# Two-layer transformer step on one core: attention scores of two heads issued as one alternating group on the two 64-row halves

## The chip, the cores and the metric

The kernel runs on one core of a Trainium2 chip, as one program with one launch. The metric is the device time of that program in microseconds (us), as the median of repeated runs, and less is better.

## The reference, cut to what matters

Two transformer blocks work on 512 tokens of width 1024. The change touches the three places where scores of queries against keys are made, all with 64 features to a head:

```python
# first block, 4 heads, each with two score maps (n = 0, 1)
scores = jnp.einsum('bhnqd,bhnkd->bhnqk', qb, kb) * scale
probs = jax.nn.softmax(jnp.where(mask, scores, -jnp.inf), axis=-1)
attn = probs[:, :, 0] - lam * probs[:, :, 1]
...
# second block, 8 index heads: which keys each query may see
dots = jnp.einsum('bqhd,bsd->bqhs', qi, k_idx)
score = jnp.einsum('bqh,bqhs->bqs', wi, jax.nn.relu(dots))
_, idx = lax.top_k(score, topk)
...
# second block, 8 attention heads over the latent keys
logits = jnp.einsum('bqhc,bqkc->bqhk', ql, c_sel) * ATT_SCALE + bias
probs = jax.nn.softmax(logits, axis=-1)
```

Everything else (projections, feed-forward layers, a gated recurrence, norms) is left as it is.

## The kernel before, in words

All activations lie in SBUF as tiles of 128 features by 512 tokens. A product in float32 is made of three products in float32r: each operand is split into a high and a low part (`split`), and high x high, high x low and low x high are added up in one PSUM bank. So a weight block of 1024 features is 24 matmuls of 512 columns.

Scores are made by `dots` (line 583): for one head, one block of 128 queries and the L keys up to that block (L = 128, 256, 384 or 512), three matmuls with 64 rows each. Two heads share a tile: one lies on rows 0 to 63, the other on rows 64 to 127. Below, A is a matmul on the lower half, B one on the upper half, and a number behind it is L / 128: A4 is a matmul of 512 columns on the lower half. A triple is the three matmuls of one head. There are 264 such matmuls:

- `attention` (line 800, phase `mixa`), four heads with two maps each: 24 matmuls of each L. Behind each triple, VectorE takes the row maximum and ScalarE the exponential.
- `select_keys` (line 1053, phase `mixb`), eight heads, L = 256, 384, 512: 24 of each. Behind each, ScalarE takes the relu and VectorE adds it to the score; then VectorE picks the greatest keys, 16 rounds of maximum and replacement to a block.
- `latent_attention` (line 1089, phase `mixb`), eight heads: 24 of each L. Behind each triple come two VectorE operations, an exponential, transposes on TensorE, a copy on ScalarE and the product with the values. `self.sm("lg", LOGITS)` takes the bank of these scores, and at most LOGITS = 3 banks hold them at a time.

PSUM has eight banks, shared by all products (`mm` for blocks of weights, `sm` for the rest). Nothing is written in the order in which it runs. `Plan.add` records each operation with a cost; `Plan.simulate` is a list scheduler over five engines, the PSUM banks and the buffers; `write` (the call is on line 444, which is why every instruction has that line in the profile) puts the operations out in the order found. Products that are ready early, above all the 16 blocks of the two gates (`w2gate`), fill TensorE between the small steps of the second block's mix. `nc.group` ties matmuls of one group into a chain: each waits its turn behind the one before it, though others may be put between them.

Of the kernel before, what the change touches and what calls it, by code (L numbers as in the profile page):

```python
# [15 lines left out]
PSUM = bass.MemoryType.PSUM  # L16
DRAM = bass.MemoryType.DRAM

P = 128
# [7 lines left out]
LEAD, PACE, LOGITS = {True: 14000, False: 6000}, 1500, 3  # L27
# [10 lines left out]
class View:  # L38
    """a tile, or a part of one, that gets its place when the program is written out"""
# [85 lines left out]
class Base:  # L125
# [5 lines left out]
    def halve(self, at):  # L131
        """from here on the columns before and behind this one are written and read apart"""
        self.at, self.parts = at, [Part(), Part()]
# [27 lines left out]
class Plan:  # L161
    """records instructions, orders them by a model of the core's engines, then writes them out"""
# [8 lines left out]
    def add(self, engine, call, args, kw):  # L171
# [41 lines left out]
        else:  # L213
# [3 lines left out]
            if engine == "tensor":  # L217
                r = all(v.base.dt == F32R for v in ins)
                wide = args[1].n
                o.cost = 3 + (128 * 2 if call == "transpose" else max(n, 2 * wide) if r else 4 * max(n, wide)) / 2.4  # L220
            elif engine == "scalar":
# [15 lines left out]
    # ordering  # L237
# [12 lines left out]
    def simulate(self, first):  # L250
        """list scheduling: sets o.start; the order of starts"""
# [195 lines left out]
class Net:  # L447
# [8 lines left out]
    # tiles  # L456
# [28 lines left out]
    # constants  # L485
    def setup(self):
# [16 lines left out]
        for _ in range(WARM):  # opens the clock gate of the array  # L503
            nc.tensor.matmul(p, self.ident, self.ident, start=True, stop=True)
# [5 lines left out]
    def later(self):  # L510
        """what the first products do not wait for"""
# [14 lines left out]
    def held(self, w, K, behind):  # L526
        """like chunk(), in slots: the parts of K blocks"""
# [21 lines left out]
    # weights: two float32r parts whose sum is the float32 weight  # L549
# [15 lines left out]
    def split(self, x, g=None, to=None):  # L565
        """x (times the column g) in two float32r parts"""
# [16 lines left out]
    def dots(self, p, q, k, s, t, L):  # L583
        """queries t..L on partitions, keys before L"""
        (qh, ql), (kh, kl) = q, k
        for i, (x, y) in enumerate(((qh, kh), (qh, kl), (ql, kh))):
            self.nc.tensor.matmul(p, x[s, t:L], y[s, :L], start=i == 0, stop=i == 2)

    def block(self, xs, w, p=None):
        """one block of 128 output features in PSUM; w: [P, K * 128] in DRAM"""  # L590
# [12 lines left out]
    def both(self, xs, ws, ps, held=None):  # L603
        """blocks of 128 output features: step by step all of them for one half of the tokens"""
# [16 lines left out]
    def tokens(self, xs, w, n, whole=False, cut=False):  # L621
        """n output features, tokens on partitions: four PSUM banks; w: [chunks, P, k * n]; whole: so many blocks of
        tokens at a time; cut: the last block by halves of the features"""
# [34 lines left out]
    # norms; with a side: for one half of the tokens  # L658
# [858 lines left out]
```

## Time and profile before

| what | value |
|---|---|
| median of the three runs | 1773.06 us (1772.69 to 1775.02) |
| span of the profiled execution | 1772.8 us; it has no other time of its own |
| TensorE (PE) busy | 1759.4 us, 99% |
| weight loads (PEld) busy | 1476.8 us, 83% |
| VectorE (DVE) busy | 1033.4 us, 58% |
| ScalarE (ACT) busy | 715.1 us, 40% |
| DMA | 162.47 MB, 92 GB/s on the mean |

The span runs from the first to the last instruction of one execution; what a run has around it is the difference to the median, 0.2 us. A matmul's busy time in the profile is longer than its turn, since the next one starts while it drains; the distance from start to start is its cost. A row that names `64*128` is a matmul with 64 rows, `128*128` one with all rows.

### The profile page before, as it was taken

To read this page: it belongs to the slowest core of one execution; us is meant where nothing else is said; L and a number is where in the kernel's file an instruction comes from. 1 tells how busy PE (TensorE), PEld (TensorE's weight loads), DVE (VectorE), ACT (ScalarE), POOL (GpSimd) and SP (SyncE) were. 2 spreads that over 40 slices of the span, in tenths; PEclk is the share of its full clock that TensorE was granted. 3 is DMA by queue.
4 is the path that set the end of the run, shared out by engine and by line. 5 is a ranking of instruction groups with operands and counts; after the bars stand their busy time and mean duration, and the time that the engine had idled before them with its cause. 6 is when DMAs were issued, how large, how long until landed. Compare 5 with 4: busy or idle time off the path is not lost.

```text
span 1772.8 us, 22576 instructions
## 1 busy us (share of the span) xinstructions
PE 1759.4 (99%) x8882; PEld 1476.8 (83%) x8882; DVE 1033.4 (58%) x1820; ACT 715.1 (40%) x1248; POOL 49.3 (3%) x68
## 2 busy tenths in 40 slices
PE   9999999999999999999999999999999999999998
PEld 7778888888888888888898888788899888888896
DVE  7886776367655432343488999553657432343475
ACT  5664444234443322322355334553345322322364
POOL 0021000000000000000010000000000000000000
PEclk9999999999999999999999999999999999999999
DMA  5212232332233223332342321013331323322331
GB/s 201 72 53 92 94 96 77 113 107 96 77 103 106 95 73 106 107 97 83 111 130 71 95 84 49 13 48 95 97 130 49 104 75 101 112 95 80 113 105 60
DMA packets 51690, 162.47 MB, mean 92 GB/s; under 512 B 5936, under 2 KB 7552, under 8 KB 51584
## 3 DMA queue, kind: packets, MB, share of 16 engines
q1 hardware_dynamic: 51584, 161.04, 28.9%
q8 instruction: 69, 1.13, 0.3%
q14 instruction: 37, 0.30, 0.1%
HBM read 158.89 MB, written 2.12 MB: 91 GB/s over the span
## 4 chain that ended last, share of the span: by engine, by line
PE 94%; DVE 4%; ACT 0%; issue 0%; DMA 0%; SPq 0%; POOL 0%; POOLq 0%; DVEq 0%; ACTq 0%
PE ffn.mm L444 41%; PE ffna.mm L444 20%; PE mixb.mm L444 15%; PE mixa.mm L444 7%; PE mixb.sm L444 5%; PE ple.mm L444 3%; DVE mixb.slot L444 2%; PE mixa.sm L444 2%; DVE mixb.m L444 0%; PE ffn.sm L444 0%; DMA mixa.wr_52:2_113<-in_w1qk 0%; SPq L444 0%; PE ple.sm L444 0%; PE fin.sm L444 0%; DVE mixa.dsum L444 0%
## 5 line engine op out<-in xcount | busy, mean ns | idle before, releaser
L444 DVE TENSOR_TENSOR ffn.slot<-ffn.slot,ffn.mm 128x512 f32<-128x512 f32 (+1 forms) x68 | 42.4, 625 | 177.2 <-PE ffn.mm L444 176.5
L444 DVE TENSOR_TENSOR ffn.slot<-ffn.mm,ffn.slot 128x512 f32<-128x512 f32 x44 | 30.3, 691 | 110.4 <-PE ffn.mm L444 109.6
L444 PE MATMUL mixb.sm<-mixb.slot,mixb.slot 128*128 128x64 f32 (+6 forms) x496 | 73.6, 308 | 1.0 <-ACT mixb.slot L444 0.5
L444 DVE TENSOR_TENSOR mixb.slot<-mixb.slot,mixb.slot 128x256 f32<-128x256 f32 (+3 forms) x143 | 67.3, 495 | 11.6 <-ACT mixb.slot L444 11.0
L444 PEld LDWEIGHTS mixb.sm<-mixb.slot,mixb.slot 128*128 128x128 f32 (+1 forms) x496 | 61.1, 190 | 12.2 <-issue 3.3
L444 DVE SCALAR_TENSOR_TENSOR ffna.slot<-ffna.slot,cols,ffna.slot 128x511 f32<-128x511 f32 x88 | 65.8, 748 | 3.1 <-ACT ffna.slot L444 1.3
L444 DVE TENSOR_TENSOR ffna.slot<-ffna.mm,ffna.slot 128x512 f32<-128x512 f32 x44 | 30.3, 689 | 46.4 <-PE ffna.mm L444 45.8
L444 ACT ACTIVATE ffn.slot<-ffn.slot 128x512 f32<-128x512 f32 (+1 forms) x68 | 39.2, 578 | 40.0 <-DVE ffn.slot L444 39.8
L444 DVE TENSOR_TENSOR ffn.slot<-ffn.slot,ffn.slot 128x512 fp32r<-128x512 f32 (+2 forms) x94 | 52.0, 562 | 5.0 <-ACT ffn.slot L444 4.6
L444 ACT COPY mixb.slot<-mixb.sm 128x128 f32<-128x128 f32 (+6 forms) x75 | 27.1, 376 | 43.3 <-PE mixb.sm L444 43.0
L444 DVE TENSOR_TENSOR ffna.slot<-ffna.slot,ffna.slot 128x512 f32<-128x512 f32 (+1 forms) x51 | 35.3, 691 | 14.7 <-ACT ffna.slot L444 13.8
L444 DVE TENSOR_TENSOR mixb.slot<-mixb.mm,mixb.slot 128x512 f32<-128x512 f32 (+1 forms) x28 | 19.3, 690 | 41.7 <-PE mixb.mm L444 40.5
L444 ACT ACTIVATE ffna.slot<-ffna.slot,cols 128x512 f32<-128x512 f32 x44 | 35.8, 815 | 2.6 <-DVE ffna.slot L444 1.9
L444 ACT CAST ffna.slot<-ffna.slot 128x512 fp32r<-128x512 f32 x22 | 13.7, 621 | 52.3 <-DVE ffna.slot L444 52.3
L444 DVE TENSOR_TENSOR h<-h,ffna.mm 128x512 f32<-128x512 f32 x16 | 11.0, 687 | 39.8 <-PE ffna.mm L444 39.8
L444 ACT ACTIVATE ffna.slot<-ffna.slot 128x512 f32<-128x512 f32 x22 | 13.9, 632 | 40.1 <-DVE ffna.slot L444 38.5
L444 DVE SCALAR_TENSOR_TENSOR mixb.slot<-mixb.sm,ffn.rr,mixb.slot 128x128 f32<-128x128 f32 (+3 forms) x32 | 17.0, 546 | 19.6 <-PE mixb.sm L444 18.5
L444 ACT CAST ffn.slot<-ffn.slot 128x512 fp32r<-128x512 f32 x44 | 27.3, 622 | 2.4 <-DVE ffn.slot L444 1.4
L444 PE MATMUL mixa.sm<-mixa.slot,mixa.slot 128*128 128x128 f32 (+5 forms) x184 | 27.9, 322 | 0.0
L444 POOL TENSOR_TENSOR ffn.rr<-ffn.rv,mhalf 128x2 f32<-128x2 f32 x8 | 6.2, 779 | 736.1 <-DVE ffn.rv L444 736.1
L444 DVE MATCH_REPLACE8 mixb.slot<-mixb.m,mixb.slot 128x256 f32<-128x256 f32 (+2 forms) x48 | 26.1, 549 | 0.0
L444 PEld LDWEIGHTS mixa.sm<-mixa.slot,mixa.slot 64*128 64x128 f32 (+1 forms) x184 | 21.3, 187 | 5.4 <-issue 2.6
(2192 smaller groups left out, 5366.3 us busy)
## 6 DMA issues: line engine op xcount, KB each, us to landing
h<-in_x SPq DMA_DIRECT2D x8, 256.0 KB, 5.9
mixb.slot<-dv SPq DMA_DIRECT2D x8, 256.0 KB, 4.3
out_y<-ple.slot SPq DMA_DIRECT2D x8, 256.0 KB, 2.0
mixa.wr_43:1_83<-in_w1qk SPq DMA_DIRECT2D x1, 512.0 KB, 4.0
mixa.wr_52:2_113<-in_w1qk SPq DMA_DIRECT2D x1, 512.0 KB, 6.7
mixa.wr_65:3_169<-in_w1v SPq DMA_DIRECT2D x1, 512.0 KB, 5.6
mixa.wr_65:4_208<-in_w1v SPq DMA_DIRECT2D x1, 512.0 KB, 5.5
mixa.wr_65:5_248<-in_w1v SPq DMA_DIRECT2D x1, 512.0 KB, 5.1
```

Source lines behind the costliest of these rows:

```text
L444: getattr(getattr(nc, engine), call)(*[real(v) for v in o.args], **{k: real(v) for k, v in o.kw.items()})
```

## The change

`dots` now takes two banks and issues both heads' triples as one group: A, B, A, B, A, B, chained. The three callers take two banks first and then work on the heads one after the other. LOGITS rises from 3 to 4. The planner's cost of a float32r matmul with 64 rows is halved, which moves other work too. (The rest of the diff takes out comments and docstrings, so that the line of `write` is now 446.)

```diff
-LEAD, PACE, LOGITS = {True: 14000, False: 6000}, 1500, 3
+LEAD, PACE, LOGITS = {True: 14000, False: 6000}, 1500, 4
...
                 o.cost = 3 + (128 * 2 if call == "transpose" else max(n, 2 * wide) if r else 4 * max(n, wide)) / 2.4
+                if r and args[1].dummy.shape[0] == 64:
+                    o.cost /= 2
...
-    def dots(self, p, q, k, s, t, L):
+    def dots(self, ps, q, k, t, L):
         (qh, ql), (kh, kl) = q, k
+        self.nc.group = self.nm("g")
         for i, (x, y) in enumerate(((qh, kh), (qh, kl), (ql, kh))):
-            self.nc.tensor.matmul(p, x[s, t:L], y[s, :L], start=i == 0, stop=i == 2)
+            for n, p in enumerate(ps):
+                s = slice(64 * n, 64 * n + 64)
+                self.nc.tensor.matmul(p[:, :L], x[s, t:L], y[s, :L], start=i == 0, stop=i == 2)
+        self.nc.group = None
...
-            for n in range(2):
-                s = slice(64 * n, 64 * n + 64)
-                p = self.sm()
-                self.dots(p[:, :L], q, k, s, b * P, L)
+            ps = [self.sm() for _ in range(2)]
+            self.dots(ps, q, k, b * P, L)
+            for n, p in enumerate(ps):
...
-            s = slice(64 * (h % 2), 64 * (h % 2) + 64)
-            p = self.sm()
-            self.dots(p[:, :L], qi[h // 2], kT, s, b * P, L)
+            if h % 2 == 0:
+                ps = [self.sm() for _ in range(2)]
+                self.dots(ps, qi[h // 2], kT, b * P, L)
+            p = ps[h % 2]
...
-            s = slice(64 * (h % 2), 64 * (h % 2) + 64)
-            p = self.sm("lg", LOGITS)
-            self.dots(p[:, :L], q[h // 2], k[h // 2], s, b * P, L)
+            if h % 2 == 0:
+                ps = [self.sm("lg", LOGITS) for _ in range(2)]
+                self.dots(ps, q[h // 2], k[h // 2], b * P, L)
+            p = ps[h % 2]
```

**TensorE, first block, second head, its last blocks of queries, before.** `sm` is a PSUM bank, the first `slot` holds keys, the second queries; the banks `sm_772` and `sm_799` are the upper half's (B3, B4), `sm_789` is the lower half's (A4).

```order
L444 MATMUL mixa.sm_772<-mixa.slot_729,mixa.slot_673 128x384
L444 MATMUL mixa.sm_772<-mixa.slot_736,mixa.slot_673 128x384
L444 MATMUL mixa.sm_777<-ident,mixa.slot_747 128x128 x4
L444 MATMUL mixa.sm_772<-mixa.slot_729,mixa.slot_695 128x384
L444 MATMUL mixa.sm_789<-mixa.slot_729,mixa.slot_673 128x512
L444 MATMUL mixa.sm_789<-mixa.slot_736,mixa.slot_673 128x512
L444 MATMUL mixa.sm_789<-mixa.slot_729,mixa.slot_695 128x512
L444 MATMUL mixa.sm_799<-mixa.slot_729,mixa.slot_673 128x512
L444 MATMUL mixa.sm_799<-mixa.slot_736,mixa.slot_673 128x512
L444 MATMUL mixa.sm_799<-mixa.slot_729,mixa.slot_695 128x512
```

The same place in the changed kernel; `sm_750` and `sm_786` are A3 and A4, `sm_752` and `sm_795` are B3 and B4.

```order
L446 MATMUL mixa.sm_750<-mixa.slot_737,mixa.slot_701 128x384
L446 MATMUL mixa.sm_752<-mixa.slot_737,mixa.slot_701 128x384
L446 MATMUL mixa.sm_750<-mixa.slot_728,mixa.slot_715 128x384
L446 MATMUL mixa.sm_752<-mixa.slot_728,mixa.slot_715 128x384
L446 MATMUL mixa.sm_786<-mixa.slot_728,mixa.slot_701 128x512
L446 MATMUL mixa.sm_795<-mixa.slot_728,mixa.slot_701 128x512
L446 MATMUL mixa.sm_786<-mixa.slot_737,mixa.slot_701 128x512
L446 MATMUL mixa.sm_795<-mixa.slot_737,mixa.slot_701 128x512
L446 MATMUL mixa.sm_786<-mixa.slot_728,mixa.slot_715 128x512
L446 MATMUL mixa.sm_795<-mixa.slot_728,mixa.slot_715 128x512
```

The two triples of 512 columns now alternate, and they stand right behind those of 384, with no transposes between.

**TensorE, latent attention, fourth block of queries, before.** `sm_9693` is A4 of the first pair of heads, `sm_9714` its B4; the rows between are transposes (`ident`) and products with the values (128x64).

```order
L444 MATMUL mixb.sm_9693<-mixb.slot_9164,mixb.slot_8816 128x512
L444 MATMUL mixb.sm_9661<-ident,mixb.slot_9643 128x128
L444 MATMUL mixb.sm_9693<-mixb.slot_9230,mixb.slot_8816 128x512
L444 MATMUL mixb.sm_9626<-mixb.slot_9176,mixb.slot_9691 128x64
L444 MATMUL mixb.sm_9626<-mixb.slot_9224,mixb.slot_9691 128x64
L444 MATMUL mixb.sm_9626<-mixb.slot_9249,mixb.slot_9691 128x64
L444 MATMUL mixb.sm_9705<-ident,mixb.slot_9631 128x128
L444 MATMUL mixb.sm_9661<-ident,mixb.slot_9643 128x128
L444 MATMUL mixb.sm_9705<-ident,mixb.slot_9631 128x128 x2
L444 MATMUL mixb.sm_9693<-mixb.slot_9164,mixb.slot_9053 128x512
L444 MATMUL mixb.sm_9714<-mixb.slot_9164,mixb.slot_8816 128x512
L444 MATMUL mixb.sm_9714<-mixb.slot_9230,mixb.slot_8816 128x512
```

The same heads in the changed kernel, from their second matmul on (the first, A4 into `sm_9705`, stands alone some rows ahead).

```order
L446 MATMUL mixb.sm_9725<-mixb.slot_9069,mixb.slot_8744 128x512
L446 MATMUL mixb.sm_9705<-mixb.slot_9248,mixb.slot_8744 128x512
L446 MATMUL mixb.sm_9725<-mixb.slot_9248,mixb.slot_8744 128x512
L446 MATMUL mixb.sm_9705<-mixb.slot_9069,mixb.slot_9085 128x512
L446 MATMUL mixb.sm_9734<-ident,mixb.slot_9679 128x128 x3
L446 MATMUL mixb.sm_9725<-mixb.slot_9069,mixb.slot_9085 128x512
L446 MATMUL mixb.sm_9652<-mixb.slot_9087,mixb.slot_9730 128x64
L446 MATMUL mixb.sm_9652<-mixb.slot_9154,mixb.slot_9730 128x64
L446 MATMUL mixb.sm_9652<-mixb.slot_9177,mixb.slot_9730 128x64
L446 MATMUL mixb.sm_9748<-mixb.slot_9110,mixb.slot_8824 128x512
```

A and B alternate, but the group still doesn't stand in one piece: other work is put between its members.

**TensorE, recurrence of the second block, before.** `mm` are matmuls of weight blocks; the first and the last row are steps of the recurrence.

```order
L444 MATMUL mixb.sm_8520<-mixb.slot_8487 128x64 x4
L444 MATMUL mixb.mm_8499<-ffn.slot_7035,mixb.wl_1280:197_8409 128x512
L444 MATMUL mixb.mm_8499<-ffn.slot_7044,mixb.wh_1280:197_8353 128x512
L444 MATMUL mixb.mm_8499<-ffn.slot_7056,mixb.wh_1280:197_8353 128x512
L444 MATMUL mixb.mm_8499<-ffn.slot_7044,mixb.wl_1280:197_8409 128x512
L444 MATMUL mixb.mm_8499<-ffn.slot_7071,mixb.wh_1280:197_8353 128x512
L444 MATMUL mixb.mm_8499<-ffn.slot_7085,mixb.wh_1280:197_8353 128x512
L444 MATMUL mixb.sm_8540<-mixb.slot_8512 32x32 x8
```

In the changed kernel nineteen matmuls of weight blocks stand ahead of the same step; the last ten of them:

```order
L446 MATMUL mixb.mm_8529<-ffn.slot_7035,mixb.wl_1311:198_8450 128x512
L446 MATMUL mixb.mm_8529<-ffn.slot_7044,mixb.wh_1311:198_8375 128x512
L446 MATMUL mixb.mm_8529<-ffn.slot_7056,mixb.wh_1311:198_8375 128x512
L446 MATMUL mixb.mm_8529<-ffn.slot_7044,mixb.wl_1311:198_8450 128x512
L446 MATMUL mixb.mm_8529<-ffn.slot_7071,mixb.wh_1311:198_8375 128x512
L446 MATMUL mixb.mm_8529<-ffn.slot_7085,mixb.wh_1311:198_8375 128x512
L446 MATMUL mixb.mm_8529<-ffn.slot_7071,mixb.wl_1311:198_8450 128x512
L446 MATMUL mixb.mm_8529<-ffn.slot_7102,mixb.wh_1311:198_8375 128x512
L446 MATMUL mixb.mm_8529<-ffn.slot_7114,mixb.wh_1311:198_8375 128x512
L446 MATMUL mixb.mm_8529<-ffn.slot_7102,mixb.wl_1311:198_8450 128x512
L446 MATMUL mixb.sm_8581<-mixb.slot_8537 32x32 x8
```

Thirteen more matmuls of 512 columns now come ahead of this step; three more ahead of the next one.

## Rows read from the trace of the kernel before

**Rows 1.** The page: busy time of each engine, share of the span, instructions

```profile
PE 1759.4 (99%) x8882; PEld 1476.8 (83%) x8882; DVE 1033.4 (58%) x1820; ACT 715.1 (40%) x1248; POOL 49.3 (3%) x68
```

**Rows 2.** The page: chain of work that ended last, by engine

```profile
PE 94%; DVE 4%; ACT 0%; issue 0%; DMA 0%; SPq 0%; POOL 0%; POOLq 0%; DVEq 0%; ACTq 0%
```

**Rows 3.** Stretches: length, busy PE, PEld, DVE, ACT, POOL; granted clock; DMA share, GB/s

```profile
952.00:1000.00 48.00, 48.00 (x213) 39.67 (x213) 47.90 (x130) 16.41 (x23) 1.19 (x3) 1.00 0.23 68
...
1034.00:1045.00 11.00, 8.97 (x61) 6.47 (x60) 11.00 (x26) 4.98 (x10) 0.00 (x0) 1.00 0.34 122
...
1127.00:1131.00 4.00, 4.00 (x18) 3.16 (x16) 0.82 (x3) 1.14 (x4) 0.00 (x0) 0.57 0.00 0
```

**Rows 4.** Groups by shape, 943 to 952 (select keys): busy us, mean ns | idle before

```profile
L444 PE MATMUL mixb.sm<-mixb.slot,mixb.slot 64*128 64x512 f32 x24 | 3.1, 389 | 0.0
L444 PE MATMUL mixb.sm<-mixb.slot,mixb.slot 64*128 64x384 f32 x24 | 2.7, 337 | 0.0
```

**Rows 5.** Groups by shape, 1107 to 1167 (latent attention)

```profile
L444 PE MATMUL mixb.sm<-mixb.slot,mixb.slot 64*128 64x512 f32 x24 | 7.1, 458 | 0.0
...
L444 PE MATMUL mixb.sm<-mixb.slot,mixb.slot 64*128 64x384 f32 x24 | 6.4, 391 | 0.0
...
L444 PE MATMUL mixb.sm<-mixb.slot,mixb.slot 64*128 64x256 f32 x24 | 4.4, 318 | 0.0
```

**Rows 6.** Timeline of PE, latent attention: start us, busy us, engine line op

```profile
1118.01 0.62 PE L444 MATMUL mixb.sm<-mixb.slot,mixb.slot 64*128 64x256 f32 x3
1118.56 0.50 PE L444 MATMUL mixb.mm<-ffn.slot,mixb.wl_1526:203_8847 128*128 128x512 f32 x1
...
1119.71 0.63 PE L444 MATMUL mixb.sm<-mixb.slot,mixb.slot 64*128 64x256 f32 x6
1120.27 0.74 PE L444 MATMUL mixb.mm<-ffn.slot,mixb.wh_1529:204_8926 128*128 128x512 f32 x2
```

**Rows 7.** Timeline of PE, later in latent attention

```profile
1159.77 0.61 PE L444 MATMUL mixb.sm<-mixb.slot,mixb.slot 128*128 128x64 f32 x4
1160.22 0.28 PE L444 MATMUL mixb.sm<-ident,mixb.slot 128*128 128x128 f32 x1
1160.43 0.50 PE L444 MATMUL mixb.sm<-mixb.slot,mixb.slot 64*128 64x512 f32 x1
1160.86 0.77 PE L444 MATMUL mixb.sm<-ident,mixb.slot 128*128 128x128 f32 x5
1161.55 1.53 PE L444 MATMUL mixb.sm<-mixb.slot,mixb.slot 64*128 64x512 f32 x9
```

**Rows 8.** Timeline of PE, select keys

```profile
943.71 2.46 PE L444 MATMUL mixb.sm<-mixb.slot,mixb.slot 64*128 64x256 f32 x23
946.54 5.27 PE L444 MATMUL mixb.sm<-mixb.slot,mixb.slot 64*128 64x256 f32 x49 [0.38 <-DVE mixb.slot L444]
951.74 0.50 PE L444 MATMUL mixb.mm<-mixb.wh_1141:183_7460,ffn.slot 128*128 128x512 f32 x1
```

**Rows 9.** Timeline of PE, first block, fourth head

```profile
109.22 1.66 PE L444 MATMUL mixa.sm<-mixa.slot,mixa.slot 64*128 64x512 f32 x6
110.81 0.50 PE L444 MATMUL mixa.mm<-mixa.slot,mixa.wl_273:13_848 128*128 128x512 f32 x1
```

**Rows 10.** Timeline of PE, recurrence

```profile
1034.46 0.39 PE L444 MATMUL mixb.mm<-ffn.slot,mixb.wl_1280:197_8409 128*128 128x512 f32 x1
1034.69 0.61 PE L444 MATMUL mixb.mm<-ffn.slot,mixb.wh_1280:197_8353 128*128 128x512 f32 x2
1036.24 1.08 PE L444 MATMUL mixb.sm<-mixb.slot 128*128 128x64 f32 x8 [0.94 <-DVE mixb.slot L444]
...
1039.31 0.45 PE L444 MATMUL mixb.sm<-mixb.slot 128*32 128x32 f32 x16 [0.55 <-DVE mixb.slot L444]
```

**Rows 11.** Timeline of PE, latent attention, near 1128

```profile
1127.87 0.77 PE L444 MATMUL mixb.mm<-ffn.slot,mixb.wh_1529:204_8926 128*128 128x512 f32 x1
1128.45 0.63 PE L444 MATMUL mixb.sm<-ident,mixb.slot 128*128 128x128 f32 x2
```

## The prediction

> **What bounds the kernel now.** First the page: TensorE is busy for 1759.4 of 1772.8 us, VectorE for 58% [rows 1]. Then the chain of work that ended last: 94% of it is TensorE, 4% VectorE [rows 2]. So a turn saved on TensorE shortens the run, except where VectorE ends the chain. The stretches show where that is: from 952 to 1000 us VectorE is busy for 47.90 of 48 us, and from 1034 to 1045 for all 11, while TensorE has 2.0 us with nothing to do [rows 3]. There the waits are on VectorE, 0.94 and 0.55 us ahead of two steps of the recurrence [rows 10].
>
> The question is then what the score matmuls cost today. The groups by shape say it: 24 matmuls of 64x512 are busy for 3.1 us in the selection of keys, and 24 of the same shape for 7.1 us in the latent attention; 64x384 takes 2.7 and 6.4 us [rows 4, 5]. One shape, two prices. The timeline shows why. At 1118.01 three matmuls of 256 columns, one head's triple, hold TensorE for 0.55 us; at 1119.71 **six** of them, both heads' triples one behind the other (A, A, A, B, B, B in the program), hold it for 0.56 us [rows 6]. Two halves of the array already work beside each other when both triples are there and ready. The change gains nothing where the triples are neighbours today; it gains where a triple stands alone, with other work behind it.
>
> **The prices.** From 946.54 to 951.74 the selection runs 49 matmuls in one piece: 2 of 256 columns, 23 of 384, 24 of 512 by the program, 21,632 columns in 5.20 us [rows 8]. Without 0.2 us for its two ends (next paragraph) that is 5.0 us for 10,816 columns on each half, 0.46 ns a column: a step (one matmul, or two on both halves) costs 0.24 us at 512 columns, 0.18 at 384, 0.12 at 256. For 128 I take 0.1, between the 0.06 that the columns give and the 0.11 of a small matmul of all rows (1159.77 to 1160.22, four) [rows 7].
>
> A *visit*, a run of 64-row matmuls between matmuls of all rows, costs something by itself. The single one at 1160.43 shows it: its forerunner takes 0.21 us to the next start where 0.11 is usual (+0.10), it takes 0.43 where its step is 0.24 (+0.19), and the five behind it take 0.69, of which 0.10 is the next entry and five turns are 0.55 (+0.04) [rows 7]. That is 0.33 us; behind it a block of 512 columns pays some 0.06 more, so I take **0.35 us a visit**.
>
> **The change, part by part.**
>
> *Latent attention.* Counted in the order, per visit, as the longer of its two halves: before, 31 visits with 73 steps, of which 50 matmuls stand alone (6 of 128 columns, 16 of 256, 16 of 384, 12 of 512); after, 28 visits with 57 steps, 18 alone (2, 6, 4, 6). So 2 steps of 128, 5 of 256, 6 of 384 and 3 of 512 go: 0.2 + 0.6 + 1.1 + 0.7 = 2.6 us. Three visits fewer: 1.05. Together **3.6 us**. All of it is on the path, since TensorE has no idle time from 1127 to 1131 [rows 3] nor elsewhere in this stage; the gates' blocks, 16 of them, wait to fill it, and the same number is left to do. The least it could be is 1.0, if the pairing comes to nothing because of waits (below).
>
> *First block.* Before, 8 visits with 10 matmuls alone (4 of 384, 6 of 512); after, 10 visits with 2 alone: 4 steps go, 0.8 us, and two visits come, 0.7. That leaves 0.1. But at 109.22 the six A4, B4 take 1.59 us [rows 9] where three steps and two ends make 0.92: B waits some 0.67 us for its bank, which ScalarE's exponential of an earlier block still reads. Three of the four heads have such a visit. In the new order B stands between A's, so a wait of B holds A too, and the transposes that stood ahead are gone: the wait can stay or double (+1.4 us in all), or go with the new order (-2.0). I take a gain of **0.4 us** with the 0.1.
>
> *Selection of keys.* 72 matmuls in one visit before and after, all paired already. The run stops for data (0.38 us idle before 946.54, and slower turns ahead of it) [rows 8]; the new order has six more matmuls of 384 columns ahead of the late tile, three steps, 0.53 us that now run in the wait. Behind it comes the stretch that VectorE fills [rows 3], which passes little of it on: **0.3 us**, between 0 and 0.5.
>
> *What the halved cost moves.* Nothing changes in number, on DMA, POOL and SP not even in order. But between steps of the recurrence the new order puts 13 and 3 more matmuls of 512 columns, at 0.23 us each [rows 10] 3.7 us, just where TensorE idles 2.0 us [rows 3]. At best all idle time near there (2.0, and some 0.4 near 1100) is filled; at worst the steps come late, VectorE waits 3.7 - 2.0 = 1.7 us for them and ends its stretch that much later. I take a gain of **1.0 us**, between +2.4 and -1.7, nearer to the row that shows idle time.
>
> *LOGITS.* One more bank lets scores run ahead; it costs the other products a bank. At nothing, as no wait on a bank shows in this stage; the rival below prices the loss of that cover. The memset and maximum of head A now come after both triples; A's triple ends no later than B's did, so nothing.
>
> Sum: 3.6 + 0.4 + 0.3 + 1.0 = 5.3 us. The span of 1772.8 becomes 1767.5; the median stands 0.2 above the span, so **1767.7 us**. A difference under 0.2%, 3.5 us, is about what a measurement of this kernel can't tell from none; the bound of faster is 1769.5.
>
> **The clock.** From 1127 to 1131 us the granted clock was 0.57 on the mean [rows 3], so 1.2 GHz for some 3.4 of the 4 us, after some twenty microseconds of small matmuls and visits; the block's matmul at 1127.87 took 0.58 us to the next start instead of 0.23 [rows 11]. It cost about 1.7 us. The changed kernel may have none, one or two such stretches there: 1.7 us either way in the range.
>
> **Rivals.**
>
> *Strict order (more gain).* If B's matmuls never passed A's, a visit A, A, A, B, B, B would have five steps, not three, and the 0.67 us at 109.22 would be no wait for a bank but lost pairing, which alternation gives back wherever it occurs. Then the first block gains 0.1 + 3 x 0.67 = 2.1 and the selection 0.5: 3.6 + 2.1 + 0.5 + 1.0 = 7.2, 1765.8 us. Against it: 0.56 us for six beside 0.55 for three [rows 6]. [...] By that rule 1119.71 would have taken 0.24 us more; the trace doesn't agree there, so 0.12.
>
> *The pairs wait (no change to speak of).* In the chain, A's second matmul can't start before B's first, so a pair needs two free banks and both heads' operands at once, and the order shows that groups don't stay in one piece: A alone, then B, A, B, A, B. If the 2.6 us of steps are eaten by such waits and the first block gains nothing, 1.0 + 0.3 + 0.3 is left, 1771.4 us. For it: the wait at 109.22 [rows 9]. Against it: the halved cost leaves the visits unpriced, so the planner still thinks TensorE faster than it is there, and what it waits for is mostly early. 0.26.
>
> *Banks run short (slower).* Four banks for scores, one or two for the outputs of a block of queries and one for a gate's block leave one or two for the transposes. If each head's transposes wait for ScalarE's copy of the head before, TensorE stalls in each of 32 heads; at 0.3 us each that is 9.6 us, net 4.3 slower, 1777.1 us. It decides against the change by more than 0.2% from (5.3 + 3.5) / 32 = 0.28 us a head. [...] For it speaks only the count of banks; against it, that the planner gives banks out by the same model as before and no wait shows from 1127 to 1131 or beside it. 0.06.
>
> That the change doesn't do what it says can be excluded by the order for the first block and the selection (all alternate); for the latent stage the 18 that stay alone are in the sum.
>
> **How the numbers follow.** Forecast 0.56, strict order 0.12, waits 0.26, banks 0.06. The forecast's own range is 1763.5 to 1770.5, nine tenths of it under 1769.5: 0.50. With 0.12 and a little of the third case, faster by over 0.2% has 0.64; same 0.30; slower 0.06. The range: all gains at their best (3.6, 2.1, 0.5, 2.4 and the clock's 1.7) give 1762.5; the third case with a stretch of low clock more reaches 1773.
>
> **What would show it.** In the groups by shape of the latent attention 64x512 falls from 7.1 to near 6 us, 64x384 from 6.4 to near 5; in the selection 3.1 and 2.7 stay. In the timeline a visit of six with the same columns takes what one of three took. Idle time of TensorE near 1035 shrinks. It would be wrong if waits on ScalarE or VectorE appear ahead of B in the visits, if idle time near 1100 grows, or if visits cost more when alternated.

## The result: slower by 0.7%, and the profile after

The changed kernel takes 1787.2 us (median of three runs of 1781.2 to 1788.28; a fourth, of 2824.72 us at a granted clock of 0.579, was disturbed and is left out, and the expectations below that say 1787.7 still count it), the kernel before 1773.32 beside it: a ratio of 1.0069, interval 1.0051 to 1.0087. The prediction said 1767.7 us, and at most 1773.0. The profiled execution has a span of 1786.6 us, 13.8 above that of before.

One figure ahead of the prediction is wrong: a run has not 0.2 but about 1.7 us around its span (1788.28 and 1786.6 here, 1.6 to 2.5 us apart in the other runs). So the execution of before that was profiled must have taken some 1774.5 us (an estimate from its span), 1.2 more than the median; its stretch of low clock, priced at 1.7 us in the prediction, can account for that. The forecast stays what it was, 5.3 us below 1773.

The page of the changed kernel, busy time and the chain by engine:

```profile
PE 1764.6 (99%) x8882; PEld 1479.2 (83%) x8882; DVE 1034.4 (58%) x1820; ACT 714.7 (40%) x1248; POOL 51.0 (3%) x68
...
PE 97%; DVE 1%; ACT 1%; DMA 0%; POOL 0%; issue 0%; SPq 0%; POOLq 0%; DVEq 0%; ACTq 0%
```

As many instructions as in [rows 1], and TensorE is busy longer, not shorter. VectorE's 4% of the chain [rows 2] has become 1%: what was to be filled near 1035 us was filled. So the loss is on TensorE itself. Its groups by shape, latent attention of the changed kernel (1095 to 1215 us):

```profile
L446 PE MATMUL mixb.sm<-mixb.slot,mixb.slot 64*128 64x512 f32 x24 | 5.9, 448 | 0.0
L446 PE MATMUL mixb.sm<-mixb.slot,mixb.slot 64*128 64x384 f32 x24 | 4.1, 375 | 0.0
L446 PE MATMUL mixb.sm<-mixb.slot,mixb.slot 64*128 64x128 f32 x24 | 3.9, 353 | 0.8 <-ACT mixb.slot L446 0.8
L446 PE MATMUL mixb.sm<-mixb.slot,mixb.slot 64*128 64x256 f32 x24 | 3.8, 328 | 0.0
```

Against [rows 5] that is 1.2 us less at 512 columns, 2.3 at 384 and 0.6 at 256. The score matmuls got cheaper as forecast. The stretches show what got dearer (length, busy PE, PEld, DVE, ACT, POOL; granted clock; DMA):

```profile
964.90:1012.90 48.00, 48.00 (x213) 39.72 (x213) 47.43 (x127) 16.87 (x23) 1.19 (x3) 1.00 0.22 69
1046.90:1057.90 11.00, 11.00 (x67) 9.03 (x66) 11.00 (x25) 4.27 (x8) 0.00 (x0) 1.00 0.12 48
54.00:62.00 8.00, 6.81 (x18) 5.01 (x19) 6.62 (x22) 4.78 (x16) 0.00 (x0) 0.57 0.19 66
78.00:82.00 4.00, 3.78 (x13) 2.54 (x13) 2.19 (x9) 2.39 (x10) 0.00 (x0) 0.57 0.34 114
102.00:106.00 4.00, 4.00 (x14) 3.17 (x13) 3.46 (x14) 2.18 (x8) 0.00 (x0) 0.57 0.02 4
1123.00:1130.00 7.00, 7.00 (x25) 5.17 (x24) 2.04 (x8) 2.04 (x4) 0.00 (x0) 0.51 0.00 0
```

The first two answer to [rows 3], 12.9 us later because the whole program is late by that much there: the 2.0 us of idle time are gone. The other four are at half clock (granted 0.50) for most of their length, 20.5 us in all (before, 3.4). There three products of 512 columns take 1.28 us from start to start (58.21 to 59.49), 0.427 each or 1.2 columns a nanosecond; at a granted clock of 1.00 three take 0.68 (299.62 to 300.30), 0.227 each or 2.26. What the prediction and the expectations write as 1.2 GHz is the first of these rates; their 2.4 GHz is the granted clock of 1.00. And TensorE waits for ScalarE where it never did, by the waits of the changed kernel's TensorE (30 to 160 us, then 1100 to 1200; total, times, longest):

```profile
PE mixa.sm L446 <- ACT mixa.slot L446: 7.3, 5, 2.7
...
PE mixb.sm L446 <- ACT mixb.slot L446: 3.3, 7, 0.7
PE mixb.sm L446 <- DVE mixb.slot L446: 0.6, 2, 0.3
```

In the kernel before, the same two windows have one wait each:

```profile
PE mixa.sm L444 <- DVE mixa.dsum L444: 0.4, 1, 0.4
...
PE mixb.sm L444 <- DVE mixb.slot L444: 0.3, 1, 0.3
```

The longest wait is at 55 us. TensorE and ScalarE of the changed kernel around it:

```profile
50.55 1.07 PE L446 MATMUL mixa.sm<-mixa.slot,mixa.slot 64*128 64x128 f32 x12
51.55 0.73 PE L446 MATMUL mixa.mm<-mixa.slot,mixa.wh_112:7_339 128*128 128x512 f32 x2
52.13 0.39 PE L446 MATMUL mixa.mm<-mixa.slot,mixa.wl_112:7_371 128*128 128x512 f32 x1
55.19 1.64 PE L446 MATMUL mixa.sm<-mixa.slot,mixa.slot 64*128 64x512 f32 x5 [2.68 <-ACT mixa.slot L446]
56.77 1.22 PE L446 MATMUL mixa.mm<-mixa.slot,mixa.wh_121:8_388 128*128 128x512 f32 x2
```

```profile
52.33 1.04 ACT L446 CAST mixa.wh_230:11_554<-mixa.wr_230:11_416 128x1024 fp32r<-128x1024 f32 x1 [4.89 <-PE mixa.mm L446]
53.39 1.28 ACT L446 ACT_TABLE_LOAD   x1
54.68 0.37 ACT L446 ACTIVATE mixa.slot<-mixa.sm,mixa.dsum 128x128 f32<-128x128 f32 x1
```

Read them together. The 512-column pair needs a bank that the first exponential (54.68) reads. ScalarE has been idle for 4.89 us, and the row maximum that the exponential takes is done at 51.51, but the exponential stands in its queue behind a weight cast of 1.04 us, which waits for a buffer that TensorE's products of the weights before free (those that start at 51.55 end at 52.28), and behind a table load of 1.28 us. TensorE has only three products left ahead of the pair, runs out of work, and waits 2.68 us. Behind that wait it runs at half clock (granted 0.50 from 55 to 61 us): two products take 1.01 us from start to start (56.77 to the next) where the two ahead of it, also right behind score matmuls, took 0.58 (51.55 to 52.13). A product shared by both programs that started at 172.2 us starts 12.9 us later; at the end it is 13.8. **So the first block lost nearly all of it**, and the second mix gave back its gain.

### The profile page after: what moved, and what is told of

Read it like the earlier page. It is cut to its first block, busy times and chain, and to the rows that moved or that the text cites. A ratio compares the mean times of both kernels' runs of the same rounds, so it can differ in the third digit from the quotient of the medians.

```text
span 1786.6 us, 22562 instructions
## 1 busy us (share of the span) xinstructions
PE 1764.6 (99%) x8882; PEld 1479.2 (83%) x8882; DVE 1034.4 (58%) x1820; ACT 714.7 (40%) x1248; POOL 51.0 (3%) x68
## 4 chain that ended last, share of the span: by engine, by line
PE 97%; DVE 1%; ACT 1%; DMA 0%; POOL 0%; issue 0%; SPq 0%; POOLq 0%; DVEq 0%; ACTq 0%
PE ffn.mm L446 40%; PE ffna.mm L446 20%; PE mixb.mm L446 18%; PE mixa.mm L446 8%; PE mixb.sm L446 5%; PE ple.mm L446 3%; PE mixa.sm L446 2%; DVE mixb.slot L446 1%; PE ffn.sm L446 0%; DMA h<-in_x 0%; ACT mixa.slot L446 0%; POOL mixb.rr L446 0%; PE ple.sm L446 0%; ACT mixb.slot L446 0%; DVE mixa.dsum L446 0%
## 5 line engine op out<-in xcount | busy, mean ns | idle before, releaser
L446 ACT CAST ffna.slot<-ffna.slot 128x512 fp32r<-128x512 f32 x22 | 13.7, 621 | 52.4 <-DVE ffna.slot L446 52.4
L446 PEld LDWEIGHTS mixa.sm<-mixa.slot,mixa.slot 64*128 64x128 f32 (+1 forms) x184 | 20.7, 195 | 13.8 <-ACT mixa.slot L446 9.6
```

Source lines behind the costliest of these rows:

```text
L446: getattr(getattr(nc, engine), call)(*[real(v) for v in o.args], **{k: real(v) for k, v in o.kw.items()})
```

## The experiments

All ratios are against the kernel before, run on the same chip. "Pairs" are the change's six matmuls in a group that the planner may part, "triples" the old form.

### One: the first block's pairs undone

```diff
-            ps = [self.sm() for _ in range(2)]
-            self.dots(ps, q, k, b * P, L)
-            for n, p in enumerate(ps):
+            for n in range(2):
+                s = slice(64 * n, 64 * n + 64)
+                p = self.sm()
+                self.dots_one(p[:, :L], q, k, s, b * P, L)
```

> The first block's heads go back to one triple after another; selection and latent attention stay paired, the planner's halved cost stays. Theory W (pairing in the first block makes A4 and B4 wait together for the banks of A1 and A2, and the clock falls behind each wait): the first block loses its 12.9 us, and 1774 to 1776 us are left, with idle time before the 512-column matmuls of the first block under 1 us in all. Rival P (the planner's halved cost, not the pairing, packs the score matmuls into one burst): the order keeps two or three visits a head, the waits on ScalarE stay, 1783 to 1788 us.

Measured: 1786.95 us, ratio 1.0080 (1.0065 to 1.0095): no better. The wait at 55 us is still there, now in front of a triple (timeline of TensorE in this experiment):

```profile
51.95 0.39 PE L446 MATMUL mixa.mm<-mixa.slot,mixa.wl_108:7_371 128*128 128x512 f32 x1
55.02 1.64 PE L446 MATMUL mixa.sm<-mixa.slot,mixa.slot 64*128 64x512 f32 x3 [2.68 <-ACT mixa.slot L446]
```

At 172 us it is 10.6 us behind. Theory W, that the first block's pairs lose the time, falls; P's range, the order by halved cost, fits.

### Two: the halved cost taken out

```diff
-                if r and args[1].dummy.shape[0] == 64:
-                    o.cost /= 2
```

> The changed kernel with the planner's full cost for 64-row matmuls; all three places stay paired. Theory W: the pairs still need two banks at once, the waits before A4 and B4 stay, 1781 to 1788 us. Rival P: the waits go, the first block is as before or 1 us better, the latent attention keeps what it had, 1770 to 1774 us.

Measured: 1796.3 us, ratio 1.0130 (1.0115 to 1.0145), worse still. The wait at 55 us is gone, but pairs in the first block now wait elsewhere (timeline of TensorE in this experiment):

```profile
68.85 1.48 PE L444 MATMUL mixa.sm<-mixa.slot,mixa.slot 64*128 64x128 f32 x18
72.12 0.49 PE L444 MATMUL mixa.sm<-mixa.slot,mixa.slot 64*128 64x512 f32 x1 [1.79 <-ACT mixa.slot L444]
72.84 1.65 PE L444 MATMUL mixa.sm<-mixa.slot,mixa.slot 64*128 64x512 f32 x5 [0.22 <-ACT mixa.slot L444]
```

Three pairs of one head run in one piece, and the fourth waits for the exponentials of the first: 8.5 us are lost by 172 us. Another 11.8 go between 1130 and 1190, where the clock is halved for 30.7 us. So the halved cost alone isn't the cause either, and P in its simple form falls too.

### Three: both, so that only the second mix is changed

> Both undone: old triples in the first block, the full cost in the planner; selection and latent attention paired, four banks for logits. Theories W and P both: the first block is as before, to 0.3 us. What is left is the latent attention alone: 33 visits and 58 steps instead of 31 and 73, which is 2.5 us less for the steps and 0.7 more for the visits, 1771 us without waits; if the waits on ScalarE at the start of the latent attention (3 us idle and 6.8 us at the low clock in the changed kernel) belong to the pairing there, 1776 to 1778 us.

Measured: 1787.71 us, ratio 1.0102 (1.0058 to 1.0146); one of the four runs took 1804.06 us at a granted clock of 0.980, the others 1785.84 to 1788.08 at 0.990. Until 1040 us it is within 0.3 us of the kernel before. Near 1112 some steps of VectorE come 2 to 3 us earlier than before and the products of a gate's block 2.7 us later: another order, and no clear lead. Then (stretches of TensorE in this experiment: length, busy, granted clock, DMA):

```profile
1095.00:1125.00 30.00, 30.00 (x202) 1.00 0.10 25
1125.00:1160.00 35.00, 34.48 (x130) 0.51 0.03 11
1160.00:1190.00 30.00, 29.00 (x193) 1.00 0.06 18
```

For 34.1 us the granted clock is 0.50; by that, half of it, 17 us of work, is lost (an estimate), and the difference goes to +13.6. TensorE is idle for 0.52 us of it. No length of wait explains this; the clock does. Against before, whose own low clock cost 1.7 us, it loses 15.4 to the clock and 1.2 to idle time; that only 13.6 are missing leaves 3.0 us for what the pairs gain (an estimate, as a remainder).

### Four: six matmuls as one planned piece

The group can't be parted any more: the planner places one operation that writes both banks, and it is written out as the six matmuls. Its planned cost is 350 ns for a visit and three steps. Selection and latent attention only; the first block is as before.

```diff
+                if call == "six":
+                    o.cost = 350 + 3 * max(n, wide) / 2.16
...
+            if call == "six":
+                p, qh, ql, kh, kl = (v.real() for v in o.args)
+                ps = (p, o.kw["accum_out"].real())
+                for i, (x, y) in enumerate(((qh, kh), (qh, kl), (ql, kh))):
+                    for n in range(2):
+                        s = slice(64 * n, 64 * n + 64)
+                        nc.tensor.matmul(ps[n], x[s], y[s], start=i == 0, stop=i == 2)
+                continue
...
+        self.nc.tensor.six(ps[0][:, :L], qh[:, t:L], ql[:, t:L], kh[:, :L], kl[:, :L], accum_out=ps[1][:, :L])
```

> Old triples in the first block at full cost; in selection and latent attention the six matmuls of a pair are planned as one piece that is never parted, at 350 ns and three steps. The order then has 16 visits with 48 steps in the latent attention instead of 31 with 73: 15 x 0.35 = 5.3 us and 25 steps, some 4 us. Theory V (visits and lone matmuls are what this stage loses): 1764 to 1766 us. Rival: a piece of six needs both banks before it starts, waits take the gain back, 1771 to 1776 us.

Measured: **1762.41 us**, ratio 0.9940 (0.9924 to 0.9957): faster than both. Its score matmuls in the latent attention (groups by shape, 1095 to 1215 us):

```profile
L452 PE MATMUL mixb.sm<-mixb.slot,mixb.slot 64*128 64x512 f32 x24 | 3.9, 426 | 0.0
L452 PE MATMUL mixb.sm<-mixb.slot,mixb.slot 64*128 64x384 f32 x24 | 3.2, 369 | 0.0
L452 PE MATMUL mixb.sm<-mixb.slot,mixb.slot 64*128 64x256 f32 x24 | 2.5, 311 | 0.0
L452 PE MATMUL mixb.sm<-mixb.slot,mixb.slot 64*128 64x128 f32 x24 | 2.2, 289 | 0.0
```

Shape by shape 3.2, 3.2 and 1.9 us less than [rows 5]. The order has 16 visits and 48 steps there, where the kernel before has 31 and 73: with the prediction's prices 15 x 0.35 = 5.3 us for the visits and 4.1 for the 25 steps (3 of 128 columns, 8 of 256, 8 of 384, 6 of 512) are 9.4 us, of 10.8 measured. A visit of six in its timeline:

```profile
1139.66 0.97 PE L452 MATMUL mixb.sm<-mixb.slot,mixb.slot 64*128 64x512 f32 x6
1140.56 0.33 PE L454 MATMUL mixb.sm<-ident,mixb.slot 128*128 128x128 f32 x1
```

It holds TensorE for 0.90 us, three steps of 0.24 and two ends. And the clock holds (stretches of this experiment):

```profile
1034.00:1045.00 11.00, 11.00 (x77) 8.98 (x77) 11.00 (x26) 5.44 (x11) 0.00 (x0) 1.00 0.20 55
1110.00:1144.00 34.00, 33.93 (x253) 27.71 (x252) 26.66 (x85) 25.70 (x88) 1.01 (x1) 1.00 0.11 33
```

What the 34 us hold is quite another mix than in the third experiment. Its two groups of 512 columns from 1125 to 1159, then three of the fourth experiment from 1110 to 1144:

```profile
L444 PE MATMUL mixb.mm<-ffn.slot,mixb.wh_1557:204_8911 128*128 128x512 f32 x4 | 2.4, 706 | 0.0
L444 PE MATMUL mixb.mm<-ffn.slot,mixb.wl_1557:204_9024 128*128 128x512 f32 x2 | 1.6, 775 | 0.0
```

```profile
L454 PE MATMUL mixb.mm<-ffn.slot,mixb.wh_1529:204_8916 128*128 128x512 f32 x16 | 6.1, 432 | 0.0
L454 PE MATMUL mixb.mm<-ffn.slot,mixb.wl_1529:204_8957 128*128 128x512 f32 x8 | 3.5, 435 | 0.0
L454 PE MATMUL mixb.mm<-ffn.slot,mixb.wh_1526:203_8764 128*128 128x512 f32 x8 | 3.3, 439 | 0.0
```

Six products of the gates' blocks in the one, 32 and more in the other; the rest are small transposes, products of 64 columns and 64-row matmuls. The next experiment tests whether that matters.

### Five: the third kernel with more large products strewn in

```diff
+            if call == "matmul" and o.args[1].dummy.shape[0] == 64:
+                x, y = o.args[1].base.tile, o.args[2].base.tile
+            for _ in range(o.spare):
+                nc.tensor.matmul(o.args[0].base.place()[:, :], x[:, :P], y[:, :T], start=True, stop=True)
...
+                if b >= 1 and c == 0:
+                    o.spare = 1
```

> The kernel of the third experiment (first block as before, full cost, pairs and four banks in the second mix), with 24 extra products of 128 rows and 512 columns, one ahead of each head's transposes in the latent attention from the second block of queries on. They write a bank that the transposes then overwrite, so the output does not depend on them. [...] Theory G: the loss of the third experiment is its 34.1 us at 1.2 GHz (17 us), which come where few products of 128 rows and 512 columns run between the short transposes and the 64-row matmuls; with such products strewn in, the clock stays at 2.4 GHz for all or most of 1110 to 1170 us (at most some 7 us low), and the time is 1787.7 - 17 + 5.1 = 1775.8 us, with 7 us still low 1779: 1772 to 1781. Theory H: the loss is waits of the pairs for banks, and the clock only follows them; the extra products take time and no wait goes: 1790 to 1794 us, with the low clock as long as before.

Measured: 1780.82 us as the median of nine runs, ratio 1.0083 (1.0047 to 1.0120), in two separate groups:

```
clock 0.999:          1779.29 1779.54 1780.08 1780.81 1780.82
clock 0.984 to 0.989: 1795.14 1795.80 1797.51 1803.85
```

One program, in one order, takes 15 us more or not, and the granted clock goes with it: at 0.989 a span of 1793 us loses 0.011 x 1793 = 20 us, at 0.999 some 2. The profiled execution is one of the second group: 0.51 from 1126 to 1161, as in the third experiment, and nine of the added products lie in that very stretch (groups by shape, 1126 to 1160):

```profile
L448 PE MATMUL mixb.sm<-mixb.slot,mixb.slot 128*128 128x512 f32 x9 | 7.1, 787 | 0.0
```

So the price of the clock is shown. That large products keep it up is not: in five runs of nine they may have, in four not; all four runs of the third experiment were at 0.990 or less, but five of nine against none of four can be chance. The added products cost some 9 us (1780 against 1787.7 - 17 = 1770.7). No run shows the 5.1 us that the expectation adds for them: at 0.227 us each, as from 299.62 us of the changed kernel, 24 would be 5.4 (an estimate). Theory G holds for the price and not for the remedy; H falls, since the runs at 0.999 are below the third experiment in the same order.

### Six: three banks for logits

```diff
-LEAD, PACE, LOGITS = {True: 14000, False: 6000}, 1500, 4
+LEAD, PACE, LOGITS = {True: 14000, False: 6000}, 1500, 3
```

> The changed kernel with three banks for logits instead of four, all else as in it. Theory F: the fourth bank lets a second pair run ahead and takes a bank from the transposes at the start of the latent attention; without it the waits at 1115 to 1122 us (about 3 us) and the 6.8 us at 1.2 GHz behind them (3.4 us) go, the first block is as in the changed kernel: 1787.7 - 6.4 = 1781 us, 1779 to 1784. Theory N: the bank decides nothing, and the loss of the change is in the first block and the order: 1786 to 1789 us. Theory S: with three banks a second pair waits for two of the first one's; 1790 us and more.

Measured: 1787.49 us, ratio 1.0075 (1.0058 to 1.0092), as the changed kernel. Its waits before the latent attention are the same ones (0.72, 0.37, 0.46, 0.57 us); the first block has the changed kernel's order. In the change as made, the fourth bank decides nothing in the median: N. The clock moved, though: in the profiled run no stretch at half clock follows those waits (granted 1.00 from 1100 to 1200), while the first block, in the same order, has 20.5 us of it where the changed kernel had 13.7.

### Seven: the halved cost alone

The kernel before, with the two lines that experiment two takes out.

> The kernel before with the halved planned cost of the 64-row matmuls and nothing else of the change: triples, three banks. Theory C: the halved cost by itself sets ScalarE's weight cast and table load ahead of the first head's exponentials, and TensorE waits about 2.7 us at 55 us and drops to 1.2 GHz behind it, as in the first experiment, whose first block (old triples too) lost 10.6 us; the second mix is within 3 us of before: 1781 to 1787 us. Rival: the order by halved cost only hurts together with grouped pairs, and the kernel is within 2 us of before: 1771 to 1775 us.

Measured: **1795.5 us**, ratio 1.0125 (1.0110 to 1.0140): 22 us slower, without one pair. TensorE's wait at 55 us is the same:

```profile
52.24 0.39 PE L446 MATMUL mixa.mm<-mixa.slot,mixa.wl_108:7_371 128*128 128x512 f32 x1
55.31 0.96 PE L446 MATMUL mixa.sm<-mixa.slot,mixa.slot 64*128 64x512 f32 x3 [2.68 <-ACT mixa.slot L446]
```

Theory C was right on the place and too low on the price: the second mix lost too, with 17 us at half clock. The full cost, 216 ns for 512 columns, is near the 0.24 us that a step is priced at; halved, it fits only where two run side by side: three matmuls of 512 columns of one head hold TensorE for 0.87 us (52.24 to 53.11 in the kernel before), six of two heads for 0.90 (experiment four). So the planner's TensorE is early, and it sets scores ahead of the exponentials that free their banks; this step is argued from the costs, and no run shows the planned times. This kernel and the first experiment have the same first block, matmul by matmul, and the same cost; with pairs in the second mix (and the fourth bank) it is 1786.95 instead of 1795.5. **At equal cost, the kernel with pairs there is 8.5 us faster**, but 4 to 5 of these are clock (0.995 against 0.993; 13.7 us at half clock against 23.9), which is no property of the pairs alone.

### Eight: one piece in all three places

> The fourth experiment (six matmuls planned as one piece with a cost of their own in selection and latent attention), and the first block's pairs as such pieces too. Theory V (visits and steps): the first block has as many visits as before (8) and five steps fewer (48 against 53), about 1.1 us: 1761.3 us, 1759 to 1763. Rival W: a pair takes two banks at once and TensorE waits for ScalarE's exponentials in the first block as it does in the second experiment, whose first block lost 8.5 us: 1766 to 1772 us.

Measured: 1762.99 us, ratio 0.9942 (0.9927 to 0.9957), as the fourth. The waits of a pair for banks are there, but small (timeline of TensorE):

```profile
51.75 0.50 PE L452 MATMUL mixa.sm<-mixa.slot,mixa.slot 64*128 64x512 f32 x1
52.89 0.96 PE L452 MATMUL mixa.sm<-mixa.slot,mixa.slot 64*128 64x512 f32 x5 [0.64 <-ACT mixa.slot L454]
```

They take back about what five steps gain. In the first block, pairing is worth nothing in this order.

### Nine and ten: the cost and the piece, apart

Nine is the eighth kernel, with the planned cost of the change's six matmuls; ten is the changed kernel, with the piece's cost shared out over its six.

```diff
-                    o.cost = 350 + 3 * max(n, wide) / 2.16
+                    o.cost = 3 * (3 + max(n, 2 * wide) / 2.4)
```

```diff
-                    o.cost /= 2
+                    o.cost = (350 + 3 * max(n, wide) / 2.16) / 6
```

> The eighth experiment (six matmuls planned as one piece in all three places), with the planned cost of a piece set to what the changed kernel plans for its six matmuls: for 512 columns 649 ns instead of 1061, for 128 columns 329 instead of 528. The 64-row visits of its order are 29 (the eighth experiment 25, the changed kernel 39). Theory C: the loss of the change comes from a planned cost that is too low, which sets the 512-column pairs so early that TensorE waits for ScalarE and VectorE, and drops to 1.2 GHz behind such waits: idle time of 5 us or more in the first block and the latent attention is back, 1773 to 1788 us. Theory P: the loss comes from pairs that the planner parts; a pair in one piece is right at any planned cost: 1761 to 1766 us, clock 0.999.

> The changed kernel, six matmuls in a group that the planner may part, with a planned cost for each of a sixth of the piece's (for 512 columns 177 ns instead of 108, for 128 columns 88 instead of 55; the full cost would be 216 and 110). The order has 46 visits of 64-row matmuls where the eighth experiment has 25. Theory C: the waits of the first head (2.7 us at 55 us) go, and the time is the eighth experiment's with 21 visits more at 0.35 us: 1763 + 7 = 1770 us, 1766 to 1774 while the clock holds, up to 10 more with a stretch of 20 us at 1.2 GHz. Theory P: parted pairs wait for ScalarE and for banks whatever is planned; the first block loses 8 us or more as in the second experiment: 1776 to 1796 us.

Measured: nine 1764.33 us, ratio 0.9951 (0.9936 to 0.9966); ten 1775.99, ratio 1.0011 (1.0001 to 1.0021). One piece stands a cost that is too low. Its waits in the ninth (30 to 160 us, then 1090 to 1200):

```profile
PE mixa.sm L454 <- DVE mixa.slot L454: 0.3, 1, 0.3
...
PE mixb.sm L454 <- ACT mixb.slot L454: 2.4, 5, 0.7
PE mixb.sm L454 <- DVE mixb.slot L454: 0.9, 1, 0.9
PE mixb.mm L454 <- DVE mixb.slot L454: 0.3, 1, 0.3
```

The latent attention waits 3.6 us, nearly as in the changed kernel (3.9), yet no stretch of that run before its last microseconds is at half clock. In the tenth the true cost takes the wait at 55 us away, and the one of experiment two is back (1.75 us at 72.94, with 6.8 us at half clock behind it). It is 11 us better than the changed kernel and 13 worse than the pieces, 7 of which are its 21 visits more, at the prediction's price. Theory P has the ninth; the tenth lies between the two, at P's low end: cost and parting both count.

### Eleven: the fourth kernel with three banks

> The fourth experiment (one piece in selection and latent attention, first block as before) with three banks for logits instead of four. A piece takes two banks at once, so that with three a second piece waits until both banks of the first are read. Theory F: the fourth bank is what lets the pieces follow one another; without it the order has a stretch of some 14 us with no product of 512 columns, and waits: 1765 to 1775 us. Rival N: other work fills these waits, 1761.5 to 1763.5 us as in the fourth experiment.

Measured: 1765.44 us, ratio 0.9956 (0.9941 to 0.9971), 3 us more than with four banks. Four waits for ScalarE come in the latent attention that the fourth experiment lacks, 0.23 us at 1144.84, 0.35 at 1147.30, 0.21 at 1162.34 and 0.68 at 1165.46; they are half of the 3 us. F, at its low end: with pieces that take two banks at once the fourth bank has a use.

### The sums

For each profiled run: idle time ahead of TensorE's instructions in the first block (30 to 160 us) and the second mix (900 to 1230), time at half clock outside the run's last microseconds, and the 64-row visits of its order.

| kernel | median us | idle, first block | idle, second mix | at half clock | visits |
|---|---|---|---|---|---|
| before | 1773.2 | 0.5 | 2.9 | 3.4 | 40 |
| changed | 1787.2 | 7.3 | 4.5 | 20.5 | 39 |
| 1 first block undone | 1787.0 | 5.6 | 4.5 | 13.7 | 41 |
| 2 full cost | 1796.3 | 5.2 | 4.1 | 41.0 | 40 |
| 3 both | 1787.7 | 0.5 | 4.1 | 34.1 | 42 |
| 5 spare products (profiled run: 1795.1) | 1780.8 | 0.5 | 4.2 | 34.1 | 42 |
| 6 three banks | 1787.5 | 7.3 | 4.9 | 20.5 | 42 |
| 7 halved cost alone | 1795.5 | 5.6 | 4.2 | 23.9 | 45 |
| 10 parted, true cost | 1776.0 | 2.3 | 2.0 | 6.8 | 46 |
| 4 one piece | 1762.4 | 0.5 | 2.3 | 0 | 25 |
| 8 one piece everywhere | 1763.0 | 1.9 | 2.3 | 0 | 25 |
| 9 one piece, halved cost | 1764.3 | 0.3 | 3.9 | 0 | 29 |
| 11 one piece, three banks | 1765.4 | 0.5 | 3.8 | 0 | 25 |

For the changed kernel against before: 8.4 us more idle time, (20.5 - 3.4) / 2 = 8.6 us of work lost to the clock, and 3.6 us less of steps and visits (by the prediction's prices) are +13.4; the spans differ by 13.8. The clock's share isn't the same in each run: the changed kernel's run of 1781.2 us had a granted clock of 0.998 where the profiled one had 0.993, and was still 7.9 us slower than before.

## Why the prediction was wrong, point by point

- **Latent attention, -3.6 us: about right.** By the groups by shape, 4.1 us less at 256 to 512 columns, though 1.4 more at 128 columns (3.9 against 2.5 before), where lone matmuls wait at 1118 and 1120 us and ten run at half clock. The row of before:

```profile
L444 PE MATMUL mixb.sm<-mixb.slot,mixb.slot 64*128 64x128 f32 x24 | 2.5, 287 | 0.0
```

The remainder of the third experiment, 3.0 us, is of that size too. What the stage lost to waits and clock stood in other terms.
- **"What the halved cost moves", -1.0 us between +2.4 and -1.7: the step that failed.** Alone it costs 22 us (experiment seven). The prediction looked for what moved near the idle time that it knew, the recurrence, and was right there: 2.0 us of idle time went. It did not look at what moved in the first block, where the halved cost leaves three products between two sets of scores and lets a weight cast and a table load stand ahead of the exponentials. The sentence that dismissed it, that what TensorE waits for "is mostly early", holds in the order of before; with the halved cost and nothing else (experiment seven) TensorE waits 2.68 us at one place.
- **First block, -0.4 us, bounds -2.1 to +1.4: wrong.** It lost 12.9. The mechanism was named (a wait of B holds A, a pair needs two free banks) and costs up to 1.8 us ahead of a pair and 0.2 inside it (experiments two and ten). But the halved cost alone loses 10.6 us here with triples (experiment one), the pairs at full cost 8.5 (experiment two), and both together 12.9: either is enough, and the two don't add up.
- **The clock, 1.7 us either way: mis-sized.** By 20.5 us at half clock it took some 10 from the changed kernel, and 17 to 20 from others (34.1 to 41.0 us). The prediction saw one stretch of 3.4 us [rows 11] and took the next for its like; that low clock came at or behind four of the new waits (2.68, 1.50, 1.95 and 0.57 us) was not in the sum. The twenty microseconds "of small matmuls and visits" ahead of that stretch hold thirteen products of 512 columns from 1117.6 to 1123.5 us.
- **LOGITS at nothing: right** for this change (experiment six).
- **Selection, -0.3 us: not seen.** The timeline of the changed kernel:

```profile
956.55 8.18 PE L446 MATMUL mixb.sm<-mixb.slot,mixb.slot 64*128 64x256 f32 x72
964.66 0.50 PE L446 MATMUL mixb.mm<-mixb.wh_1169:183_7460,ffn.slot 128*128 128x512 f32 x1
```

From its first matmul to the product behind it, the visit takes 8.11 us against 8.03 before, the wait of 0.38 included [rows 8], and the program is as late behind it as ahead of it (12.9 us).
- **Rivals.** Strict order fell: alternation gave the selection nothing, and the 0.5 us it forecast there would have come from lost pairing. "The pairs wait" had the mechanism and a fifth of the price (3.7 us off the forecast, where 19.5 came), and gave no reason for counting the halved cost's 1.0 us at 0.3. "Banks run short" had the sign, but in the latent attention one set of transposes waits for ScalarE (0.56 us at 1148.30), not thirty-two.

## What to carry to other kernels

Where a planner orders the work, a changed cost is a change of the whole program: compare every stage in which it moves something, and look on each engine for what now stands ahead of the work that frees a bank (here a cast of 1.04 us and a table load of 1.28 ahead of an exponential). If two matmuls are cheap only when they run side by side (here six in 0.90 us where three took 0.87), make them one planned operation with their joint, measured cost, rather than giving each half a price that holds only beside the other: that turned a loss of 14 us into a gain of 11. And a wait of TensorE can cost more than its length: in the changed kernel 8.4 us of idle time came with 8.6 us of work lost to the clock, though in the ninth experiment 3.6 us of waits in the latent attention came with none.

## What the runs showed of the hardware

- **The low clock lasted while TensorE was busy.** In the third experiment the granted clock stayed at 0.50 for 34.1 us while TensorE was busy for 34.48 of 35 us. In this time it ran transposes of 128 columns, products of 64 columns, 64-row matmuls and six products of 512 columns. The clock rose at 1159.7 us, 4.7 us behind the last three of the six (1153.30 to 1154.95); the same three at 1140.00 to 1145.28 were followed by no rise, and in the profiled run of the fifth experiment nine more of them left the stretch as long. What raised it is open.
- **It fell at short waits, and not at every one.** It fell at or behind waits of 2.68, 1.50, 1.95 and 0.57 us in the changed kernel, and at one of 0.52 us in the third experiment; in the kernel before it fell at 1127.2 us, 23 us behind the last wait of over 0.2 us; a wait of 0.86 us at 98 us was followed by a fall in experiment seven and by none in experiment one, in the same order. In the fifth, one program had it in four runs of nine. What sets it off within such a stretch is open.
